# Heads' projections: Strassen over 16 K tiles in place of 14 for 27 pairs of column tiles

## Chip, core and metric

The kernel runs on one core of a Trainium2 chip. A core has a matrix engine (TensorE, PE on the profile's page; PEld is its loading of weights), three others that compute (VectorE or DVE, ScalarE or ACT, GpSimd or POOL), and SyncE (SP), which here issues the transfers of weights. Each engine runs its own list of instructions strictly in order and waits on semaphores for the others. TensorE writes its products into PSUM, a small memory of eight banks; everything else lies in SBUF, and the weights come from HBM by DMA. The metric is the time of one execution in device microseconds (us); lower is better.

## The reference

Two layers of a decoder with D = 2048, for 512 prompt tokens and 8 sample tokens, all in fp32. The part that matters here:

```python
h = rmsnorm(x, norm_g)
z = h @ w_in                          # 2048 x 8192
b_c, c_c, x_c, g_c, q, k, v, g_r = split_projection(z)
conv_y, new_buf = short_conv(c_c * x_c, conv_buf, conv_w)
y_conv = b_c * conv_y * silu(g_c)
q, k = rope(q), rope(k)               # 4 heads of 256
o, new_S = retention(q, k, v, ret_S, log_gamma)
y_ret = groupnorm(o) * gn_g * silu(g_r)
x = x + concat([y_conv, y_ret]) @ w_out
x = x + sigmoid(x @ w_pg) * (p_i @ w_ple)
```

After the two layers comes a final rmsnorm.

## The kernel before

**Tiling.** Activations lie transposed, as 16 K tiles of 128 partitions (features) by 520 columns (512 prompt tokens and 8 samples). The columns are used in two halves of 260, LEFT and RIGHT. A product with a weight matrix is made for two column tiles of the weights (256 output features) at a time; this is a *pair* (`pair`), and a layer has 32 pairs of `w_in` (16 for the heads: q, k, v and gate of four heads, then 16 for the convolution), 8 of `w_out` and 8 of `w_pg`.

**Three matmuls for one.** fp32 accuracy comes from splitting every operand into a high part, rounded to the engine's fast format, and the rest. `split_w` does it for weights: ScalarE writes the high part (L229) and VectorE the difference (L230). `mm3` then makes three matmuls (L247 to L249), each 128x128 weights by 260 columns.

**Strassen.** A pair has 2 x 16 weight tiles and 16 x 2 activation tiles (K tiles by halves). `plain` multiplies them directly: 16 x 2 x 2 x 3 = 192 matmuls. `strassen(x, src0, src1, s)` takes the first `s` K tiles as a 2 x 2 block problem (even and odd K tiles, two halves, two weight tiles), in Winograd's form with seven products of q = s / 2 tiles each in place of eight. The sums of activations, t1 to t4, are made once and kept (`operand_sums`, L413 to L416, then split in `split_sums`); the sums of weights are made for each pair on VectorE (`add`, L319: four sums of q tiles). The K tiles from `s` to 16, if any, are multiplied directly at the end of the pair: `parts` loads them (L222) and four `product` calls use them. In all a pair costs 7 x q x 3 + (16 - s) x 4 x 3 matmuls: 171 with s = 14, 168 with s = 16.

Banks of PSUM for pairs are five. A pair holds three (a, b, d) and, only when s < 16, a fourth, c, into which ScalarE copies b (`copy(... c, b)`, L307), so that the last K tiles can add to it. With s = 16 that copy goes to SBUF, and two of the later copies become sums on VectorE with one operand in PSUM.

**Weights on their way.** Raw weights land in a ring of 32 tiles of 128 columns (`raw_ring`), taken in steps of 8 tiles (steps of 4 for pieces of up to 4 tiles). A block of q tiles is loaded, summed and split in chunks of at most four tiles: with q = 7 as 3 + 4 (instructions of 384 and 512 columns), with q = 8 as 4 + 4. The last two K tiles of s = 14 come as two more loads of 256 columns. Split weights go into a second ring of 60 tiles (`split_ring`), which is how far ScalarE and VectorE can run ahead of TensorE.

**What sets the order.** The tables `HEADS` and `CONVS` give s for each pair of `w_in`, in the order in which the pairs run; `OUT_ROWS` and `GATES` do so for the rest. The host packs the weights by the same tables. A scheduler at build time orders the instructions of each engine, by priorities and its own estimate of times. Between a pair's products stand other steps: `rope` (L753 to L758), `silu`, the sample states (`sample_step`, L777 to L785) and, in pieces taken from the list `later`, retention itself (`steps`, L870 to L1001). `Operands.need` sees to it that a pair finds the sums of all its K tiles: `need(n)` builds until s / 2 sums are there. `fill` builds more of them when slots of SBUF are free.

Of the kernel before, what the change touches and what calls it, by code (L numbers as in the profile page):

```python
# [49 lines left out]
EARLY = 6  # L50


HEADS = [[0, 0, 0, 8] + [14] * 12, [0] + [14] * 15]
CONVS = [[14] * 2 + [16] * 13 + [14]] * 2
OUT_ROWS = [[0, 8, 16, 16, 16, 16, 16, 0]] * 2

# [135 lines left out]
def trunk_kernel(  # L192
# [370 lines left out]
    def norm_g(l, k):  # L563
        return vec[:, 16 * l + k : 16 * l + k + 1]
# [97 lines left out]
    def from_dram(src):  # L662
        def load(k):
            t = get()
            SIDE.dma_start(t, src[k])
            return t

        return load

    xs = []  # L670
    X = Operands(HEADS[0][2:] + CONVS[0], from_dram(xT), gain=lambda k: norm_g(0, k))
    X.todo = [t for t in ((i, False, True) for i in range(max(X.rows) // 2))]
# [43 lines left out]
    for l in range(DEPTH):  # L716
# [456 lines left out]
        if not tail:  # L1173
            X = Operands(HEADS[l + 1] + CONVS[l + 1], next_in, RESERVE_NEXT, gain=lambda k, l=l: norm_g(l + 1, k))
        for m in range(0, KT - tail, 2):
# [303 lines left out]
```

## Time and profile before

| | |
|---|---|
| runs | 2172.50, 2166.74, 2170.08 us; median 2170.08 |
| the profiled execution | 2172.46 us, its span 2170.4 us |
| granted TensorE clock over the span | 0.998 |
| ACT busy over the span | 1266.2 us (58%) |
| POOL busy over the span | 430.5 us (20%) |
| DMA over the span | 387.31 MB, mean 178 GB/s |

The profile is of one execution, and the 2.1 us between its time and its span lie before its first and after its last instruction. In the span the first layer's heads run until about 380 us and its convolution until about 700 us; the output and gate projections follow until about 1118 us, where the second layer's heads take up, until about 1466 us; its convolution ends at about 1780 us. A row of a group of instructions ends with their busy time, the mean of one in ns, and then the engine's idle time before them with what ended it. A row of the windows gives busy us of each engine in a stretch, with the number of instructions in brackets.

### The profile page before, as it was taken

To read this page: it belongs to the slowest core of one execution; us is meant where nothing else is said; L and a number is where in the kernel's file an instruction comes from. 1 tells how busy PE (TensorE), PEld (TensorE's weight loads), DVE (VectorE), ACT (ScalarE), POOL (GpSimd) and SP (SyncE) were. 2 spreads that over 40 slices of the span, in tenths; PEclk is the share of its full clock that TensorE was granted. 3 is DMA by queue.
4 is the path that set the end of the run, shared out by engine and by line. 5 is a ranking of instruction groups with operands and counts; after the bars stand their busy time and mean duration, and the time that the engine had idled before them with its cause. 6 is when DMAs were issued, how large, how long until landed. Compare 5 with 4: busy or idle time off the path is not lost. (4 is left out here: it accounts for less than half of the span.)

```text
span 2170.4 us, 48198 instructions
## 1 busy us (share of the span) xinstructions
PE 2148.5 (99%) x17861; PEld 2142.9 (99%) x17861; DVE 1895.7 (87%) x3849; ACT 1266.2 (58%) x2661; POOL 430.5 (20%) x746
## 2 busy tenths in 40 slices
PE   9999999999999999999999999999999999999998
PEld 9999999999999999999999999999999999999998
DVE  8889989898999987987897988989999998878884
ACT  8656556655555555655765655565655555456565
POOL 2313222211001211210212222231111022121011
PEclk9999999999999999999999999999999999999999
DMA  8556675545543645645645566665464455566455
GB/s 288 176 169 196 185 215 183 186 152 172 156 134 120 228 156 186 217 153 161 214 144 174 172 210 193 190 195 183 147 182 145 127 155 199 181 212 195 127 169 192
DMA packets 182861, 387.31 MB, mean 178 GB/s; under 512 B 25888, under 2 KB 56352, under 8 KB 182624
## 3 DMA queue, kind: packets, MB, share of 16 engines
q1 hardware_dynamic: 129136, 213.77, 31.8%
q0 software_dynamic: 53056, 169.84, 23.8%
q8 instruction: 140, 2.29, 0.4%
q14 instruction: 97, 0.79, 0.1%
q10 hardware_dynamic: 432, 0.61, 0.1%
HBM read 318.96 MB, written 65.15 MB: 177 GB/s over the span
## 5 line engine op out<-in xcount | busy, mean ns | idle before, releaser
L247 PE MATMUL ps_g<-slot,split 128*128 128x260 f32 x5465 | 1532.3, 284 | 9.7 <-ACT slot L307 3.4
L248 PE MATMUL ps_g<-slot,split 128*128 128x260 f32 x5465 | 1535.1, 283 | 0.3 <-DVE slot L555 0.3
L249 PE MATMUL ps_g<-slot,split 128*128 128x260 f32 x5461 | 1520.5, 283 | 0.5 <-DVE split L230 0.5
L229 ACT ACTIVATE split<-raw 128x512 fp32r<-128x512 f32 (+2 forms) x1347 | 778.2, 596 | 587.6 <-DVE raw L319 205.6
L247 PEld LDWEIGHTS ps_g<-slot,split 128*128 128x128 f32 x5465 | 1024.5, 188 | 12.9 <-ACT slot L307 4.2
L248 PEld LDWEIGHTS ps_g<-slot,split 128*128 128x128 f32 x5465 | 1029.3, 188 | 0.5 <-DVE slot L555 0.5
L249 PEld LDWEIGHTS ps_g<-slot,split 128*128 128x128 f32 x5461 | 1020.3, 188 | 0.8 <-DVE split L230 0.7
L230 DVE TENSOR_TENSOR split<-raw,split 128x512 fp32r<-128x512 f32 (+2 forms) x1346 | 844.1, 647 | 176.5 <-PE ps_g L248 85.4
L319 DVE TENSOR_TENSOR raw<-raw 128x512 f32<-128x512 f32 (+1 forms) x660 | 426.2, 656 | 28.1 <-DMA raw<-wi 18.4
L307 ACT ACTIVATE slot<-ps_g 128x260 f32<-128x260 f32 x336 | 127.2, 381 | 142.5 <-PE ps_g L249 127.2
L551 ACT ACTIVATE slot<-slot 128x520 fp32r<-128x520 f32 (+1 forms) x212 | 109.1, 562 | 41.8 <-DVE slot L414 10.2
L552 DVE TENSOR_TENSOR slot<-slot,slot 128x520 fp32r<-128x520 f32 (+1 forms) x212 | 122.9, 609 | 4.3 <-ACT slot L551 4.2
L782 POOL DMA_DIRECT2D o_rets<-slot x64 | 35.3, 552 | 350.6 <-DVE slot L781 131.8
L307 DVE TENSOR_TENSOR slot<-ps_g,slot 128x260 f32<-128x260 f32 x168 | 70.5, 421 | 7.3 <-PE ps_g L249 4.9
L870 POOL DMA_DIRECT2D slot<-hs x64 | 46.1, 723 | 126.5 <-DVE split L230 35.5
L815 POOL DMA_DIRECT2D hs<-slot x64 | 35.6, 556 | 137.9 <-DVE slot L756 59.6
L747 DVE TENSOR_TENSOR slot<-slot,slot 128x520 f32<-128x520 f32 x80 | 55.4, 692 | 4.6 <-DMA o_rets<-slot 3.7
L1059 POOL DMA_DIRECT2D slot<-x1s x76 | 40.8, 538 | 88.0 <-PE ps_g L249 28.3
L781 DVE SCALAR_TENSOR_TENSOR slot<-slot,vs,slot 128x256 f32<-128x256 f32 x128 | 55.9, 477 | 2.6 <-ACT slot L777 2.3
L1209 POOL DMA_DIRECT2D x2s<-slot x30 | 16.3, 545 | 203.4 <-DVE slot L1204 202.5
L771 POOL DMA_DIRECT2D slot<-sret x64 | 35.5, 555 | 106.4 <-ACT split L229 43.4
L772 POOL DMA_DIRECT2D slot<-kq x64 | 34.9, 547 | 109.2 <-DVE slot L877 20.5
(217 smaller groups left out, 1727.0 us busy)
## 6 DMA issues: line engine op xcount, KB each, us to landing
raw<-wi SPq DMA_DIRECT2D x377, 256.0 KB, 3.9
raw<-wo SPq DMA_DIRECT2D x128, 256.0 KB, 5.6
raw<-wg SPq DMA_DIRECT2D x122, 256.0 KB, 4.2
raw<-wi SPq DMA_DIRECT2D x136, 192.0 KB, 4.0
slot<-x1s POOLq DMA_DIRECT2D x76, 260.0 KB, 5.0
slot<-sret POOLq DMA_DIRECT2D x64, 256.0 KB, 4.0
hs<-slot POOLq DMA_DIRECT2D x64, 256.0 KB, 3.9
slot<-hs POOLq DMA_DIRECT2D x64, 256.0 KB, 5.1
```

The costliest lines, as they stand in the source:

```text
L229: S.activation(hi, raw, AF.Copy)
L230: V.tensor_tensor(lo, raw, F(hi), SUB)
L247: PE.matmul(out, wh, xh, start=start, stop=False, skip_group_check=more)
L248: PE.matmul(out, wh, xl, start=False, stop=False, skip_group_check=more)
L249: PE.matmul(out, wl, xh, start=False, stop=stop, skip_group_check=more)
L307: fn(*args)
L319: V.tensor_tensor(out[:, n], x[:, n], y[:, n], op)
L551: keep(S.activation(hi, src[:, n], AF.Copy))
L552: V.tensor_tensor(lo, src[:, n], F(hi), SUB)
L747: V.tensor_tensor(out[:, n], v, table[:, n], MUL)
L781: keep(V.scalar_tensor_tensor(st[:, c], k, vs[:, h, e, b : b + 1], st[:, c], MUL, ADD))
L870: SIDE.dma_start(t[:, :512].rearrange("p (m n) -> p m n", m=2), src)
```

## The change

One table is changed. In layer 0 the pairs 4 to 15 of the heads, in layer 1 the pairs 1 to 15, are computed with s = 16; 12 + 15 = 27 pairs.

```diff
-HEADS = [[0, 0, 0, 8] + [14] * 12, [0] + [14] * 15]
+HEADS = [[0, 0, 0, 8] + [16] * 12, [0] + [16] * 15]
 CONVS = [[14] * 2 + [16] * 13 + [14]] * 2
 OUT_ROWS = [[0, 8, 16, 16, 16, 16, 16, 0]] * 2
```

In the built program TensorE has 81 matmuls fewer (17746 for 17827), VectorE 54 instructions fewer (3797 for 3851), ScalarE 81 fewer (2585 for 2666), SyncE 54 loads fewer with the same bytes. Among the forms: the splits (L229, L230) of 256 columns go from 66 to 12 and those of 384 from 249 to 60 on each of the two engines, and those of 512 go up by 189; the sums of weights (L319) of 384 columns go from 140 to 32, those of 512 from 520 to 628; copies from PSUM to PSUM (L307) go from 121 to 94. The order of the convolutions, the output and the gate projections stays as it was but for a few rows at the seams.

On SyncE, where the first layer's heads begin (`raw<-wi` is a load of `w_in` into the ring), the rows of the difference are:

```order
 L222 DMA raw<-wi 128x512 x4
+L312 DMA raw<-wi 128x512 x96
+L312 DMA raw<-wi 128x384
+L312 DMA raw<-wi 128x512
 L312 DMA raw<-wi 128x384 x2
 L312 DMA raw<-wi 128x512 x2
 L312 DMA raw<-wi 128x384
-L312 DMA raw<-wi 128x512
-L312 DMA raw<-wi 128x384
-L312 DMA raw<-wi 128x512
-L222 DMA raw<-wi 128x256 x2
```

The mixed loads, with two of 256 columns at each pair's end (L222), have become 96 loads of 512 columns in a row, eight for each of the twelve pairs; the first two pairs of the convolution, which keep s = 14, follow with the old sizes.

On ScalarE, in the first layer beside retention's first state (`ps_st`, `decay`), where one pair ends and the next begins, before:

```order
L307 ACTIVATE ps_g<-ps_g 128x260
L954 ACTIVATE slot_178_2016<-ps_st,decay 128x512
L229 ACTIVATE split<-raw 128x512
L229 ACTIVATE split<-raw 128x384
L307 ACTIVATE ps_g<-ps_g 128x260
L229 ACTIVATE split<-raw 128x512
L989 ACTIVATE slot_179_2041<-ps_o,shift,rstp 128x256 x2
L777 ACTIVATE slot_174_1911<-slot_174_1911,vec 128x512
L229 ACTIVATE split<-raw 128x256 x2
L229 ACTIVATE split<-raw 128x384
L307 ACTIVATE slot_187_2082<-ps_g 128x260 x2
```

and of the change at the same place:

```order
L307 ACTIVATE ps_g<-ps_g 128x260
L229 ACTIVATE split<-raw 128x512 x2
L954 ACTIVATE slot_178_1994<-ps_st,decay 128x512
L229 ACTIVATE split<-raw 128x512 x2
L989 ACTIVATE slot_179_2019<-ps_o,shift,rstp 128x256 x2
L777 ACTIVATE slot_174_1915<-slot_174_1915,vec 128x512
L229 ACTIVATE split<-raw 128x512 x3
L307 ACTIVATE slot_187_2059<-ps_g 128x260 x2
L229 ACTIVATE split<-raw 128x512 x2
L307 ACTIVATE slot_188_2060<-ps_g 128x260
```

The second copy from bank to bank (b into c) and the two splits of 256 columns are gone from the pair's end; the copies of results into slots stand in the same order, among splits that are all of 512 columns.

On VectorE, before the first of the changed pairs, the eighth sum of activations moves. Before, it stands among the rotations of the first q and k (`slot_150` and `slot_151` are its two halves):

```order
L230 TENSOR_TENSOR split<-raw,split 128x512
L755 TENSOR_TENSOR slot_65_721<-slot_66_724,slot_70_734 128x520
L413 TENSOR_TENSOR slot_150_1583<-slot_148_1577 128x260
L415 TENSOR_TENSOR slot_151_1584<-slot_149_1579,slot_148_1577 128x260
L755 TENSOR_TENSOR slot_67_727<-slot_68_730,slot_70_734 128x520
```

and with the change it stands some thirty rows later, behind the transpose for the samples (L842), where the pair ahead of the first changed pair adds up its result (L307, out of bank c; `slot_141` and `slot_142` are the sum's halves):

```order
L413 TENSOR_TENSOR slot_141_1402<-slot_139_1396 128x260
L307 TENSOR_TENSOR slot_112_1109<-ps_g,slot_112_1109 128x260
L319 TENSOR_TENSOR raw<-raw 128x512
L230 TENSOR_TENSOR split<-raw,split 128x512
L414 TENSOR_TENSOR slot_141_1402<-slot_140_1398,slot_141_1402 128x260
L415 TENSOR_TENSOR slot_142_1403<-slot_140_1398,slot_139_1396 128x260
```

In the second layer the eighth sum keeps its place, before the rotation's tables are scaled (L729).

## Prediction

> **What bounds the kernel now.** I read the page's head first, then the chain of work that ended last.
>
> ```profile
> span 2170.4 us, 48198 instructions
> PE 2148.5 (99%) x17861; PEld 2142.9 (99%) x17861; DVE 1895.7 (87%) x3849; ACT 1266.2 (58%) x2661; POOL 430.5 (20%) x746
> PE 43%; DMA 2%; issue 2%; DVE 1%; ACT 1%; POOL 0%; DVEq 0%; POOLq 0%; ACTq 0%
> ```
>
> TensorE is busy for 99% of the span, and it is the largest share of the chain. A busy PE need not be a PE at its pace, so the second thing to read is how far apart its matmuls start: the timeline of TensorE in an undisturbed stretch.
>
> ```profile
> 299.83 0.28 PE L247 MATMUL ps_g<-slot,split 128*128 128x260 f32 x1
> 300.79 0.28 PE L249 MATMUL ps_g<-slot,split 128*128 128x260 f32 x1
> ```
>
> Eight matmuls start between these two: 0.96 / 8 = 0.120 us each, with no gap. That is the price of a matmul here, not the 0.28 us that one lasts, since they overlap. VectorE, at 87%, is the only other engine near its limit. Whether it or TensorE sets the pace is a question for each stage, so the third view is the busy time in windows (columns: PE, PEld, DVE, ACT, POOL, clock, DMA).
>
> ```profile
> 100.00:380.00 280.00, 280.00 (x2344) 280.00 (x2343) 252.74 (x565) 168.00 (x368) 76.47 (x133) 1.00 0.60 190
> 380.00:700.00 320.00, 319.26 (x2667) 319.09 (x2666) 290.95 (x586) 177.22 (x362) 46.23 (x70) 1.00 0.49 153
> 700.00:740.00 40.00, 36.03 (x284) 35.42 (x283) 38.16 (x82) 27.63 (x80) 13.20 (x25) 0.96 0.76 250
> 1118.00:1466.00 348.00, 346.00 (x2887) 345.00 (x2886) 306.58 (x673) 201.98 (x450) 90.33 (x155) 1.00 0.60 187
> 1466.00:1780.00 314.00, 313.56 (x2619) 313.02 (x2619) 289.75 (x581) 176.56 (x364) 45.80 (x70) 1.00 0.49 153
> ...
> 1700.00:1780.00 80.00, 80.00 (x672) 80.00 (x671) 75.49 (x155) 45.63 (x95) 10.73 (x10) 1.00 0.41 124
> ```
>
> The first and fourth rows are the heads of the two layers, where the changed pairs stand; the second and fifth are mostly convolution, which already runs 13 of its 16 pairs with s = 16. TensorE is full in all four. VectorE has 252.74 / 280 = 90.3% in the first heads and 306.58 / 348 = 88.1% in the second. **TensorE bounds the heads**, and VectorE has 27 and 41 us left there.
>
> **The change part by part.** *Matmuls.* A pair goes from 171 to 168, so 27 x 3 = 81 are removed, as the program's counts say. They stand at the pair's end in an unbroken row of matmuls: 81 x 0.120 = **-9.7 us**. [...] The measured spacing, 0.120 us, decides, and the sum goes by it.
>
> *VectorE and ScalarE.* The groups by form give the durations.
>
> ```profile
> L230 DVE TENSOR_TENSOR split<-raw,split 128x512 fp32r<-128x512 f32 x1031 | 690.9, 685 | 152.9 <-PE ps_g L248 81.9 <-ACT split L229 53.8 <-issue 7.2
> L230 DVE TENSOR_TENSOR split<-raw,split 128x384 fp32r<-128x384 f32 x249 | 136.1, 550 | 15.3 <-ACT split L229 8.0 <-PE ps_g L248 3.6 <-ACT slot L551 1.6
> L230 DVE TENSOR_TENSOR split<-raw,split 128x256 fp32r<-128x256 f32 x66 | 27.0, 417 | 8.3 <-ACT split L229 8.1
> L319 DVE TENSOR_TENSOR raw<-raw 128x512 f32<-128x512 f32 x520 | 351.9, 684 | 13.7 <-DMA raw<-wi 6.6 <-DMA raw<-wo 4.6
> L319 DVE TENSOR_TENSOR raw<-raw 128x384 f32<-128x384 f32 x140 | 76.9, 550 | 14.4 <-DMA raw<-wi 11.8 <-DMA raw<-wg 2.1
> ...
> L229 ACT ACTIVATE split<-raw 128x512 fp32r<-128x512 f32 x1032 | 632.8, 627 | 468.6 <-DVE raw L319 184.7 <-PE ps_g L249 181.2 <-PE ps_g L248 50.3
> L229 ACT ACTIVATE split<-raw 128x384 fp32r<-128x384 f32 x249 | 127.3, 518 | 77.7 <-PE ps_g L248 24.4 <-DVE raw L319 20.9 <-PE ps_g L249 17.9
> L229 ACT ACTIVATE split<-raw 128x256 fp32r<-128x256 f32 x66 | 27.3, 415 | 41.2 <-DMA raw<-wi 35.8 <-PE ps_g L248 3.0 <-PE ps_g L249 1.9
> L307 ACT ACTIVATE ps_g<-ps_g 128x260 f32<-128x260 f32 x121 | 45.1, 373 | 17.4 <-PE ps_g L249 16.9
> ```
>
> On each engine 189 splits of 384 columns become 512, and 54 of 256 go; on VectorE 108 sums of 384 also become 512. VectorE: 189 x (0.685 - 0.550) - 54 x 0.417 + 108 x (0.684 - 0.550) = 25.5 - 22.5 + 14.5 = **+17.5 us busy**, 0.65 a pair. ScalarE: 189 x 0.109 - 54 x 0.415 - 27 x 0.373 = 20.6 - 22.4 - 10.1 = -11.9 us; at 58% that is no bound. VectorE's instructions overlap a little when they follow each other:
>
> ```profile
> 1131.90 0.68 DVE L230 TENSOR_TENSOR split<-raw,split 128x512 fp32r<-128x512 f32 x1
> 1132.50 0.69 DVE L755 TENSOR_TENSOR slot<-slot,slot 128x520 f32<-128x520 f32 x1
> 1133.11 0.55 DVE L230 TENSOR_TENSOR split<-raw,split 128x384 fp32r<-128x384 f32 x1
> 1133.58 0.55 DVE L319 TENSOR_TENSOR raw<-raw 128x384 f32<-128x384 f32 x1
> ```
>
> From start to start it is 0.60 for 512 columns and 0.47 for 384, 0.08 less than the duration; a removed instruction then frees only 0.34. By these the work added is 297 x 0.13 - 54 x 0.34 = 20 us, so 17.5 is the lower end.
>
> Is there room? In the first heads VectorE goes to (252.74 + 12 x 0.65) / (280 - 12 x 0.36) = 260.5 / 275.7 = 94.5%, in the second to (306.58 + 15 x 0.65) / (348 - 15 x 0.36) = 316.3 / 342.6 = 92.3%. The nearest rows: at 92.3% the second convolution let TensorE wait 0.44 us in 314, and at 94.4% its last 80 us none. What hides the added work is VectorE's idle time, and the ring of 60 split tiles that smooths its bursts. Bounds for what TensorE pays: 0 by those rows, 17.5 if none of the idle can be used. I take **+1.0 us**, near the rows of the convolution, and a little over them because the heads come in bursts (rotations, gates, sample states).
>
> *The pair's end.* With s = 16 the late loads of the last K tiles and the copy into bank c are gone. What they do shows at 1270 us, in the second heads:
>
> ```profile
> 1269.92 0.42 ACT L229 ACTIVATE split<-raw 128x256 fp32r<-128x256 f32 x1 [1.37 <-DMA raw<-wi]
> 1270.87 0.37 ACT L307 ACTIVATE ps_g<-ps_g 128x260 f32<-128x260 f32 x1
> 1271.29 0.39 PE L247 MATMUL ps_g<-slot,split 128*128 128x260 f32 x1 [0.90 <-ACT ps_g L307]
> ...
> PE ps_g L247 <- ACT ps_g L307: 2.9, 4, 1.1
> PE ps_g L247 <- ACT ps_g L307: 1.8, 3, 0.9
> ```
>
> ScalarE sits 1.37 us before a split of 256 columns whose load is late; behind it in its queue is a copy between banks, and TensorE waits 0.90 us for that. The last two rows are such waits of TensorE in the whole span and in the second heads: 2.9 and 1.8 us. Of these only what hangs on the removed loads and the 27 copies goes: 0 to 1.8 us, and a loss is excluded by no row but would be a wait of the kind counted above. I take **-1.0 us**, half, since the copy from a into d stays.
>
> *Banks.* Two of five stay free with s = 16 instead of one, so the next pair starts its second product without waiting for a bank. The row of the second convolution (0.44 us lost) already contains that; nothing more is booked.
>
> *The eighth sum* of activations is now needed by the first changed pair. Its price is known:
>
> ```profile
> L413 DVE TENSOR_TENSOR slot<-slot 128x260 f32<-128x260 f32 x48 | 20.2, 422 | 7.5 <-DMA slot<-x1s 6.2 <-ACT slot L465 0.8 <-PE ps_g L249 0.3
> L552 DVE TENSOR_TENSOR slot<-slot,slot 128x520 fp32r<-128x520 f32 x148 | 99.0, 691 | 3.6 <-ACT slot L551 3.6
> ```
>
> Four steps of 0.42 and two splits of 0.69 are 3.1 us, paid before as well. In the first layer it stands behind the closing sum of the pair ahead. From there the order has ten VectorE rows to its first split, some 5 us at 0.34 to 0.60 each, while TensorE still has three products of that pair's last tiles, the first product of the new pair and seven tiles of its second: 36 + 24 + 21 = 81 matmuls, 9.7 us. So it is covered by 4.7 us; uncovered it would cost up to 3.1. In the second layer its place is unchanged. I book 0.
>
> Weights: the same bytes in 54 fewer loads; 0.
>
> Sum: -9.7 + 1.0 - 1.0 = **-9.7 us**. Against the profiled execution, 2172.46, that is 2162.8; it lies 2.4 above the median of the runs, 2170.08, from which the same sum gives 2160.4. A new median should lie near the latter; I say **2161.0**, leaning a little to the former.
>
> **The rivals.** *The gain is given back in waits.* VectorE's bursts make TensorE wait, in the first heads above all (94.5%). One wait of the size seen at 1271 us, 0.9 us, in each of the 12 pairs there: +10.8, so 2170.1 - 9.7 + 10.8 = 2171.2. For it: the row 700 to 740, where VectorE has 95.4% and TensorE lost 4 of 40 us. Against it: that row is a seam, with chains that the heads lack, and the 94.4% row lost nothing. Waits can cost more than themselves:
>
> ```profile
> 720.00:740.00 20.00, 17.11 (x128) 16.70 (x127) 18.16 (x39) 12.09 (x39) 5.59 (x11) 0.91 0.76 265
> 740.00:760.00 20.00, 20.00 (x169) 19.98 (x168) 16.18 (x33) 9.79 (x21) 3.94 (x8) 1.00 0.55 175
> PE ps_g L247 <- ACT split L229: 1.9, 1, 1.9
> ```
>
> Here 41 matmuls, 4.9 us, are missing against the next row, with 2.9 us of waits (20.00 - 17.11) and a granted clock of 0.91. [...] Chance 0.25.
>
> *VectorE becomes the bound: slower.* If its idle time in the heads cannot be used, because each idle stretch waits for something that TensorE needs too, its added work lengthens the stage: +17.5 us, with no gain from TensorE: 2187.6. It decides from the point where VectorE's 27 and 41 us of idle in the two stages stay what they are. Against it: in all stages with s = 16 VectorE works at 91 to 94% under a full TensorE, and the first row of its splits waits 81.9 us for TensorE, which is work done too early. Chance 0.06.
>
> *More than the sum.* All 2.0 us that TensorE lost in the second heads go and nothing is added: 2158.4. For it: VectorE's and ScalarE's waits for late loads (35.8 us before the 256 splits) go. Chance 0.12.
>
> *The change does nothing*, 2170: excluded by the counts of matmuls but for chance; 0.01. That leaves 0.56 for the forecast, 2157 to 2166.
>
> **How the numbers follow.** A measurement of this kernel tells about 0.3% from no change: 6.5 us, so faster is below 2163.6 and slower above 2176.6. Faster: nine tenths of the forecast and the better case, 0.50 + 0.12 = 0.62. Slower: the VectorE rival and a tenth of the waits, 0.06 + 0.02 = 0.08. The rest, 0.30, is the same. The range goes from the better case less the 3.3 us by which the lowest run lay under the median, 2155, rounded down to 2154, to the waits case plus half the runs' spread (2.9), 2174; it leaves out the slower rival.
>
> **What would show it.** Right: 81 matmuls fewer, 100 to 376 us and the second heads still with TensorE at 99% or more, VectorE at about 94 and 92% there, no splits of 256 columns in the heads and no wait of TensorE on a copy between banks behind one. Wrong: TensorE waiting on splits of VectorE in the heads, VectorE's idle there unchanged, a first changed pair that waits on the eighth sum, or new waits or a lower clock at the seams near 700 and 1780 us.

## The result and the profile after

The change is slower, by 0.8%. Its median is 2186.64 us (four runs, 2185.05 to 2187.76) against 2168.77 for the kernel before beside it (four runs, 2166.74 to 2172.5): a ratio of 1.008, 95% interval 1.0062 to 1.0097. The forecast was 2161.0 with a range of 2154 to 2174; one of the rivals, VectorE as the bound, had been worked out at 2187.6. The experiments below ask whether it came out right for its own reason.

The head of the page and the engines' shares of the chain that ended last, after:

```profile
span 2184.6 us, 47639 instructions
PE 2147.4 (98%) x17780; PEld 2137.7 (98%) x17780; DVE 1915.4 (88%) x3795; ACT 1257.1 (58%) x2580; POOL 431.9 (20%) x746
PE 74%; DMA 4%; DVE 3%; ACT 2%; issue 2%; POOL 0%; DVEq 0%; POOLq 0%; SPq 0%; ACTq 0%
```

The span grew by 14.2 us although 81 matmuls are gone (17861 to 17780). VectorE's busy time rose by 19.7. The page's 98% of TensorE hides the loss; the windows show it (columns: PE, PEld, DVE, ACT, POOL, clock, DMA share, GB/s):

```profile
100.00:380.00 280.00, 272.14 (x2249) 270.56 (x2248) 253.00 (x523) 158.70 (x325) 76.45 (x130) 0.99 0.58 187
380.00:700.00 320.00, 318.76 (x2660) 318.35 (x2659) 294.52 (x597) 179.71 (x368) 48.98 (x74) 1.00 0.50 154
700.00:740.00 40.00, 38.95 (x320) 38.32 (x319) 39.03 (x83) 29.25 (x83) 10.66 (x20) 1.00 0.72 249
1118.00:1466.00 348.00, 336.85 (x2765) 333.69 (x2764) 309.73 (x626) 190.72 (x390) 85.99 (x147) 0.99 0.57 180
1466.00:1780.00 314.00, 313.64 (x2622) 313.22 (x2621) 289.12 (x581) 175.58 (x363) 46.65 (x71) 1.00 0.49 155
```

TensorE now waits 7.9 us in the first heads (280.00 - 272.14; before 0) and 11.2 in the second (before 2.0); the convolutions wait 0.4 us more in all, and the seam at 700 us 2.9 less. The counts of matmuls show the whole loss: 95 and 122 fewer start in the two stages than before (2344 - 2249, 2887 - 2765), which at 0.120 us is 11.4 and 14.6 us. So 17.0 of these 26.0 us are new waits (7.9 and 9.1), and the rest are matmuls that start further apart; the granted clock is 0.99 in both stages, where it was 1.00. VectorE did not rise to the 94.5% and 92.3% of the forecast: it stands at 253.00 / 280 = 90.4% and 309.73 / 348 = 89.0%. Its idle time there is 27.0 and 38.3 us, where it was 27.3 and 41.4. **The added work did not go into VectorE's idle time. The stages became longer instead.**

What TensorE waits for, whole span (total, times, longest), after:

```profile
PE ps_g L247 <- ACT split L229: 10.2, 6, 3.4
PE ps_g L249 <- DVE split L230: 5.9, 7, 1.7
PE ps_g L247 <- ACT slot L307: 4.4, 6, 1.5
PE ps_g L247 <- ACT ps_g L307: 3.1, 2, 1.5
```

Waits on splits, 1.9 and 0.5 us before, are now 16.1. Most of them (10.2 us) name ScalarE, not VectorE. One place from the timeline shows why that doesn't acquit VectorE:

```profile
257.14 0.63 ACT L229 ACTIVATE split<-raw 128x512 fp32r<-128x512 f32 x1 [2.10 <-DMA raw<-wi]
257.80 0.69 DVE L230 TENSOR_TENSOR split<-raw,split 128x512 fp32r<-128x512 f32 x1 [0.95 <-ACT split L229]
...
257.82 0.39 PE L247 MATMUL ps_g<-slot,split 128*128 128x260 f32 x1 [3.44 <-ACT split L229]
```

TensorE waits for ScalarE, ScalarE for a load, and VectorE for ScalarE; the load itself was issued late, because its block is free only when a VectorE sum (L319) has read it: such a sum ended at 251.93 us, and SyncE issued a load at 251.96. It is a ring of engines, and the name at its end is that of the last link. The waits of ScalarE in the first heads (100 to 380 us) say the same:

```profile
ACT split L229 <- PE ps_g L249: 43.3, 38, 6.0
ACT split L229 <- DVE raw L319: 20.6, 17, 3.0
ACT split L229 <- DMA raw<-wi: 13.4, 7, 4.1
...
ACT slot L307 <- DMA hs<-slot: 4.5, 1, 4.5
```

Before, the lines of the splits were:

```profile
ACT split L229 <- PE ps_g L249: 19.1, 33, 1.8
ACT split L229 <- PE ps_g L248: 18.3, 28, 2.2
ACT split L229 <- DVE raw L319: 13.6, 16, 1.6
ACT split L229 <- DMA raw<-wi: 8.9, 6, 3.4
```

A split that waits for TensorE waits for a place in the split ring, which the matmuls of L248 or L249 read last. Together these two lines were 37.4 us, and they are 43.9 now (L248 stands at 0.6). The waits for VectorE's sums and for loads grew by half.

### The profile page after: what moved, and what is told of

Same layout as the page of the kernel before. It is cut to its first block, busy times and chain, and to the rows that moved or that the text cites. A ratio compares the mean times of both kernels' runs of the same rounds, so it can differ in the third digit from the quotient of the medians.

```text
span 2184.6 us, 47639 instructions
## 1 busy us (share of the span) xinstructions
PE 2147.4 (98%) x17780; PEld 2137.7 (98%) x17780; DVE 1915.4 (88%) x3795; ACT 1257.1 (58%) x2580; POOL 431.9 (20%) x746
## 4 chain that ended last, share of the span: by engine, by line
PE 74%; DMA 4%; DVE 3%; ACT 2%; issue 2%; POOL 0%; DVEq 0%; POOLq 0%; SPq 0%; ACTq 0%
PE ps_g L247 23%; PE ps_g L249 23%; PE ps_g L248 23%; DMA raw<-wi 2%; DVE split L230 1%; ACT split L229 1%; DMA o_rets<-slot 1%; DMA hs<-slot 1%; ACT slot L551 1%; DVE slot L552 0%; PE ps_p L247 0%; PE ps_p L249 0%; PE ps_p L248 0%; DVE raw L319 0%; DMA x2s<-slot 0%
## 5 line engine op out<-in xcount | busy, mean ns | idle before, releaser
L247 PE MATMUL ps_g<-slot,split 128*128 128x260 f32 x5434 | 1525.2, 284 | 20.7 <-ACT split L229 10.2
L248 PE MATMUL ps_g<-slot,split 128*128 128x260 f32 x5434 | 1528.1, 283 | 0.3 <-DVE slot L555 0.3
L249 PE MATMUL ps_g<-slot,split 128*128 128x260 f32 x5434 | 1515.8, 283 | 6.1 <-DVE split L230 5.9
L229 ACT ACTIVATE split<-raw 128x512 fp32r<-128x512 f32 (+1 forms) x1292 | 778.2, 620 | 608.4 <-PE ps_g L249 245.1
L249 PEld LDWEIGHTS ps_g<-slot,split 128*128 128x128 f32 x5434 | 1017.2, 189 | 8.2 <-DVE split L230 8.2
L248 PEld LDWEIGHTS ps_g<-slot,split 128*128 128x128 f32 x5434 | 1024.1, 189 | 0.5 <-DVE slot L555 0.5
L230 DVE TENSOR_TENSOR split<-raw,split 128x512 fp32r<-128x512 f32 (+1 forms) x1292 | 849.4, 675 | 182.8 <-PE ps_g L248 87.3
L319 DVE TENSOR_TENSOR raw<-raw 128x512 f32<-128x512 f32 (+1 forms) x660 | 439.7, 677 | 26.0 <-DMA raw<-wi 21.6
L307 ACT ACTIVATE slot<-ps_g 128x260 f32<-128x260 f32 x336 | 126.9, 383 | 141.3 <-PE ps_g L249 119.9
L307 DVE TENSOR_TENSOR slot<-ps_g,slot 128x260 f32<-128x260 f32 x168 | 70.6, 420 | 5.4 <-PE ps_g L249 3.5
```

The source lines that it names most:

```text
L229: S.activation(hi, raw, AF.Copy)
L230: V.tensor_tensor(lo, raw, F(hi), SUB)
L247: PE.matmul(out, wh, xh, start=start, stop=False, skip_group_check=more)
L248: PE.matmul(out, wh, xl, start=False, stop=False, skip_group_check=more)
L249: PE.matmul(out, wl, xh, start=False, stop=stop, skip_group_check=more)
L307: fn(*args)
```

## The experiments

Eighteen kernels were run. Each is compared with some runs of the kernel before on the same chip; "against before" is the difference of the two medians. The change itself stands at +17.9 us.

### Is it the late load, or a ring that is too small?

The block of `w12` in the raw ring is given back later, together with that of `w11` and behind it, so that the next pair's first load goes where `w11` lay:

```diff
-        raw_ring.put(w12)
         step(4)
...
-        raw_ring.put(w11)
+        raw_ring.put(w11, w12)
```

> The changed kernel, with w12's block of the raw ring given back together with w11's and behind it, so that the next pair's first block goes where w11 lay and not where w12 lay. No work is added or left out. Theory late loads (the next pair's first load waits for the sum that reads w12 last, and lands 4 us too late): the waits of TensorE at 257 and 1333 us go, and the time falls by 5 us or more, to 2182 or less. Theory VectorE (its 17.5 us of added work set the pace): within 3 us of the 2186.6 of the change. Theory split ring (chunks are split too near to their use, because the places they go to are freed late): within 3 us of it too.

2184.97 us, +16.0, ratio 1.007 (1.0055 to 1.0086). TensorE's waits in this run:

```profile
PE ps_g L247 <- ACT slot L307: 7.2, 8, 2.9
PE ps_g L249 <- DVE split L230: 5.5, 6, 1.7
...
PE ps_g L247 <- ACT split L229: 2.8, 2, 2.5
```

The wait on ScalarE's splits fell from 10.2 to 2.8 us, as it should, yet the time fell by 1.9 only (17.9 - 16.0): other waits rose in its place, that on copies out of PSUM from 4.4 to 7.2. In the heads TensorE still waits 6.8 and 8.3 us (before this edit 7.9 and 11.2). By these figures late loads are not the main part of the loss.

The same line moved in the kernel before, as a control for what a mere reordering costs:

> Control: the kernel before with the same order of giving back w12 and w11. In the heads s = 14 puts the late pieces of the last K tiles into w12's place, so theory late loads expects within 6 us of the kernel before, either way; the other theories expect no change.

2176.76 us, +7.8, ratio 1.0034 (1.0022 to 1.0046). An edit that adds no work costs 8 us here, so differences of this size between orders prove little by themselves. It also leaves open how much late loads cost: if the edit by itself costs the change as much as its control, the gain is not 1.9 us but 9.7, of the 27.6 that are to be explained (17.9 and the 9.7 us that the matmuls should have saved).

Rings of other sizes, with s = 16 (`RAW` 32 to 40 and `SPLIT` 60 to 56; then `SPLIT` 60 to 64):

> The changed kernel with a raw ring of 40 tiles (five blocks for a pair that uses four) and a ring of split weights of 56 tiles for 60. Theory late loads: the first load of a pair can start a whole product earlier, 2165 to 2178. Theory VectorE: 2187, no change. Theory split ring: the smaller ring makes it worse, 2190 or more.

> The changed kernel with a ring of split weights of 64 tiles for 60 (an even eight chunks of four tiles, high and low). Theory split ring: the waits on splits near 161, 166, 1237 and 1243 us go, 2170 to 2182. Theory VectorE: 2183 to 2187. Theory late loads: 2184 to 2188.

2199.06 us, +30.1, ratio 1.0135 (1.0118 to 1.0152), and 2183.94, +15.0, ratio 1.0065 (1.0048 to 1.0082). Four places fewer in the split ring, with a deeper ring of raw weights, cost 12 us; four more bring 3. The first run changed two rings, so it does not show which of them cost the 12 us; a larger split ring does not mend the loss. With 64 places the waits moved again:

```profile
PE ps_g L247 <- ACT slot L307: 14.4, 12, 2.3
...
PE ps_g L249 <- DVE split L230: 3.0, 6, 0.8
```

### Is it VectorE's work? Adding it to the kernel before

One VectorE instruction of 128x512 on a tile that nothing else uses, written into the middle of each of the 27 pairs (18.5 us in all), and then two:

```diff
+        def more_work():
+            for _ in range(1):
+                V.tensor_tensor(extra, extra, extra, MUL)
...
+            if X.rows[m // 2 - skipped] > 8:
+                middle.append(more_work)
```

> The kernel before (s = 14) with one more VectorE instruction of 128x512 in the middle of each of the 27 pairs: 27 x 0.685 = 18.5 us of added VectorE work on a tile that nothing reads, as much as the change adds; loads, ScalarE, matmuls and banks as before. Theory VectorE (its idle time in the heads cannot be used): 2169 + 18 = 2187, at least 2178. Theory structure (what the s = 16 pair lacks or orders otherwise, not the amount of VectorE work): 2166 to 2173.

> The same with two such instructions in each pair, 37 us of added VectorE work. Theory VectorE: 2206. Theory structure: under 2180.

2179.73 us, +10.1, ratio 1.0044 (1.003 to 1.0059), and 2192.48, +22.9, ratio 1.01 (1.0082 to 1.0117). But the scheduler did not leave the instructions in the pairs. Nothing waits for them, and it moved them to the front. In the run with one:

```profile
L806 DVE TENSOR_TENSOR extra<-extra x27: 678/685/696, 1.4 to 81.8; 128x512 f32<-128x512 f32 x27
```

The last two times are the first and the last start: all 27 started before 82 us, and none in the stretch of the changed pairs, from 100 us on, or in the second layer. With two a pair, the 54 ran from 1.4 to 176.6 us. So neither run prices the work where the change puts it. What they show is read from the windows, first before:

```profile
0.00:100.00 100.00, 97.14 (x780) 95.53 (x781) 84.74 (x166) 71.66 (x150) 30.06 (x61) 1.00 0.71 236
```

and with one instruction a pair:

```profile
0.00:100.00 100.00, 96.81 (x773) 95.05 (x774) 92.60 (x176) 66.87 (x139) 23.95 (x50) 1.00 0.66 215
100.00:380.00 280.00, 273.55 (x2274) 272.15 (x2273) 249.68 (x559) 164.50 (x365) 81.14 (x141) 1.00 0.61 193
1118.00:1466.00 348.00, 345.75 (x2878) 344.09 (x2877) 305.95 (x667) 199.36 (x447) 88.33 (x151) 1.00 0.59 184
```

Up to 100 us VectorE is busy 7.9 us longer, for 18.5 us of added work; so some of its other work was pushed on into the first heads. There it had 27 us idle, and it did not use them to catch up: it is busy for 249.68 of 280 us, no more than the 252.74 of the kernel before, and TensorE waits 6.5 us where it waited for nothing. The second heads, to which nothing was added, wait 2.3 us (before 2.0). So a VectorE that enters the first heads late stays late, and part of the idle time there is not to be had. How much a pair's own added work costs, these runs don't show.

### Is it VectorE's work? Taking it away

These kernels no longer compute the reference's output; they only show what the work costs. First, the sample states' reductions, 63 us of VectorE's work by their durations, in both kernels. In the trace of the kernel before, 74 of the 128 reductions (L785) run in the two heads' windows and the rest in the convolutions; the page's busy time of VectorE falls by 34.0 us in the change and 30.4 in the control, not by 63:

```diff
+    G.memset(osum, 1.0)
...
-            for e in range(2):
-                c = slice(256 * e, 256 * e + 256)
-                V.tensor_tensor_reduce(k, st[:, c], kb[:, :256], 1.0, 0.0, MUL, ADD, osum[:, e, h, b : b + 1])
```

> The changed kernel without the sample states' reductions over the key axis (the sample part of the output is left out): 128 instructions of 0.415 us and as many short reads of 0.08 us, about 63 us of VectorE work less, some 1.2 us for each pair of the heads, twice what the change adds there. Theory VectorE: the waits of TensorE in the heads go, 2160 to 2166. Theory structure: 2178 or more.

> Control: the kernel before without the same reductions. It waits only 2 us in the second heads and 2 more elsewhere in projections: 2163 to 2168 under both theories; what s16_less_vector lies under or over it is the change without VectorE's load: 9.7 us under by theory VectorE, over it by theory structure.

2166.06 us, -3.6, ratio 0.9981 (0.9969 to 0.9994), and for the control 2165.3, -4.3, ratio 0.9979 (0.997 to 0.9989). The change is no longer slower than its control: 0.8 us above it instead of 17.9. But it should now be 9.7 below. In the first heads of the change:

```profile
100.00:380.00 280.00, 278.06 (x2324) 277.64 (x2323) 252.91 (x475) 166.88 (x339) 79.06 (x134) 1.00 0.59 193
```

VectorE is as busy as ever, 252.91 us: what was taken away is filled at once with more of the pairs' work. TensorE still lacks 1.9 us here, and 5.0 in the second heads (343.00 of 348).

Then the work in the pair itself: one of the weights' sums, or two, left out of the heads' pairs.

```diff
...
-        add(w21, w12, w21, SUB)
+        if not cut:
+            add(w21, w12, w21, SUB)
...
```

> The change, with the weights' sum for the sixth product left out of every Strassen pair of the heads (two instructions of 128x512; the sixth product takes what stands in that block, so q, k, v and the gates are not the reference's). VectorE has 37 us less to do, 19 less than the kernel before has. Theory A, VectorE's load, which counts in the pair where the splits are due: no waits of TensorE in the heads, 2155 to 2160, 5 to 10 below its control. Theory C, a rest that does not hang on VectorE's load: 2162 to 2170, within 3 of its control.

> The control: the kernel before with the same sum left out of the same pairs (33 us less on VectorE). TensorE waits 2 us in its heads, so both theories give 2163 to 2168, near the 2165.3 of the control with less sample work.

> The change, with the sums for the sixth and the second product left out of the heads' pairs (73 us less on VectorE). Theory A: as fast as TensorE goes, 2153 to 2158, 8 to 11 below its control. Theory C: still within 3 of its control, 2162 to 2168.

> The control: the kernel before with the same two sums left out (67 us less on VectorE): 2162 to 2167, since TensorE has only some 2 us of waits in the heads to win back.

With one sum less: 2161.75 us, -8.1, ratio 0.9966 (0.9953 to 0.9979); control 2167.39, -2.4, ratio 0.999 (0.998 to 0.9999). With two less: 2161.92, -7.9, ratio 0.9964 (0.9952 to 0.9976); control 2165.48, -4.3, ratio 0.998 (0.9971 to 0.999). So one sum a pair, 36.7 us of VectorE's work by its durations, buys the change 26 us, and the control 2.4: the change goes from 17.9 slower than the kernel before to 8.1 faster, 5.6 below its control. The heads of the change without one sum:

```profile
100.00:380.00 280.00, 279.74 (x2338) 279.33 (x2337) 250.88 (x524) 166.32 (x339) 78.60 (x135) 1.00 0.60 194
1118.00:1466.00 348.00, 343.31 (x2864) 342.08 (x2863) 304.01 (x626) 198.51 (x410) 88.83 (x153) 1.00 0.57 186
```

In the first heads TensorE is full again; in the second it still waits 4.7 us. Theory A, VectorE's load, met its number of 5 to 10 below the control with one sum, though not its time of 2155 to 2160; with two the medians differ by 3.6 and not by 8 to 11. What TensorE itself does then agrees better, by the heads of those two pages (change, then control):

```profile
PE 2138.0 (99%) x17780; PEld 2131.8 (99%) x17780; DVE 1857.0 (86%) x3685; ACT 1260.6 (58%) x2580; POOL 431.3 (20%) x746
```

```profile
PE 2145.5 (99%) x17861; PEld 2140.9 (99%) x17861; DVE 1848.7 (85%) x3739; ACT 1275.1 (59%) x2661; POOL 430.1 (20%) x746
```

TensorE is busy 7.5 us less for 81 matmuls less. The gain on TensorE is there, and it comes out when VectorE has less to do: against its control the change goes from 17.9 us slower to 0.8 slower, 5.6 faster and 3.6 faster. Leaving out a sum takes a link out of the chain to the splits as well as work; the reductions, which stand outside that chain, bring back 17.1 us all the same.

### Are the result slots needed too early?

With s = 14 the second product's result waits in bank c; with s = 16 it goes to a result slot at once. In the change one of ScalarE's copies waits 4.5 us for a slot that is still being written out to hs, once in each layer (the last row above of its waits). Two runs were to remove that wait: the second product's result in a free bank again, and one slot more (`NSLOT` 75 to 76).

```diff
-        c = banks.get() if s < KT else None
+        c = banks.get() if s < KT or bank else None
...
             copy(z1[:, LEFT], a)
+            if s == KT:
+                plus(z1[:, RIGHT], c, z1[:, LEFT])
+                copy(z0[:, LEFT], d)
+                banks.put(c)
+                c = None
```

> The change, but in the heads' pairs the second product's result waits in a free fourth bank, as it did with s = 14, and not in the pair's result slot; after the fifth product it is added to that one's copy. One copy of 128x260 on ScalarE more in a pair, the first use of the second result slot later by three products; VectorE's work is the same. Theory A, VectorE's load alone: within 4 us of the change, 2181 to 2190, and the wait of 4.5 us of ScalarE's copies on a slot that is still being written out to hs (once in each layer, at 306 and 1382 us) may go without effect. Theory B, result slots that are needed earlier: this wait of 4.5 us falls under 2 in both layers, and the time falls by 5 to 10 us, to 2175 to 2180.

> The change with 76 slots in place of 75, which is all that fits. Theory B, slots asked for before their transfer out is done: the waits of ScalarE on hs and o_rets (14.9 us in the second heads) fall by half or more, and the time by 3 to 10 us, to 2175 to 2182. Theory A, VectorE's load alone: no change, 2182 to 2190. The order shifts by itself, which the control with another release order priced at up to 8 us, so a fall of less than that speaks for B only together with the shorter waits.

2188.86 us, +19.8, ratio 1.0089 (1.0071 to 1.0106), and 2214.23, +45.2, ratio 1.0212 (1.019 to 1.0235). With the bank, the second heads have this left of the wait, and the first none:

```profile
ACT slot L307 <- DMA hs<-slot: 2.2, 1, 2.2
```

But the same copies now wait for slots on another way out, the sample states' (`o_rets`), in the first heads

```profile
ACT slot L307 <- DMA o_rets<-slot: 6.3, 3, 2.7
```

and 6.4 us in the second, where these lines were 0.4 and 3.7 in the change. The copies' waits on slots were moved and not removed, so this run does not decide on theory B. The run with one slot more does remove most of them: the waits of all of ScalarE's instructions on both ways out fall from 11.8 to 4.0 us in the first heads (78 to 380 us) and from 16.3 to 2.2 in the second. Yet it is 27 us slower than the change, and TensorE's waits on ScalarE's splits grew:

```profile
PE ps_g L247 <- ACT split L229: 17.4, 13, 3.3
```

Fewer waits on slots brought no time, which speaks against theory B, as far as one order can. Why one slot more costs 27 us is open: it shifts which slot every later tile gets, and so the order, but no run takes that apart.

### Can it be mended?

GpSimd is busy for 20% of the span. It was given the sum for the sixth product, in both kernels:

```diff
...
-        add(w21, w12, w21, SUB)
+        add(w21, w12, w21, SUB, G if side else V)
...
```

> The change, but in the 27 changed pairs the sum for the sixth product (w12 - w21, two instructions of 128x512 a pair) runs on GpSimd: 54 x 0.68 = 36.7 us less on VectorE, in the pair itself and not in the steps between pairs. Theory A, VectorE's load: 2184 less 20 to 27, so 2157 to 2166, below the kernel before; VectorE at 90% of 100 to 380 us or less, TensorE at 279 of 280. Theory C, that a rest of some 10 us does not come from VectorE's load: no lower than 2166. Rival: GpSimd takes over 4 us for one such sum (no row shows one; its queue issues transfers as well), the sum comes late for the sixth product, and the time goes above 2186.

> The control: the kernel before with the same sum of its changed pairs on GpSimd (54 instructions, one of 512 and one of 384 columns less on VectorE in a pair, 33 us). TensorE has no waits in the heads to win back, so 2165 to 2170, and 0 to 5 below the kernel before. Theory A: the change with its sum on GpSimd lies 5 to 10 below this one; theory C: within 3 us of it. Rival: the sum comes late on GpSimd, both are slower by the same amount.

2210.9 us, +41.9, ratio 1.0206 (1.0169 to 1.0243); control 2200.39, +31.4, ratio 1.0141 (1.012 to 1.0162). The groups by form, in the run with s = 16:

```profile
L230 DVE TENSOR_TENSOR split<-raw,split 128x512 fp32r<-128x512 f32 x1220 | 842.3, 708 | 160.0 <-PE ps_g L248 86.8 <-ACT split L229 55.9 <-issue 7.2
...
L319 POOL TENSOR_TENSOR raw<-raw 128x512 f32<-128x512 f32 x55 | 93.1, 1695 | 95.8 <-DVE split L230 86.6 <-DVE shift L985 4.8 <-DVE mv L982 2.2
```

The rival held in another way than expected. One of a sum's two instructions takes 1.70 us on GpSimd in the mean, so the sum takes 3.4 and not over 4; ScalarE's splits wait 19.8 us for these sums. And VectorE's own splits rose from 684 to 708 ns, and its busy time from 1915.4 to 1935.0 us although 55 instructions had left it. The 75 splits of 512 columns that ran at the same time as one of GpSimd's sums took 1.05 us in the mean and up to 2.6, and of the others none took more than 0.70. Why they take longer there, the trace does not show.

Last, longer instructions: each weights' sum in one of 1024 columns instead of two of 512 (`CHA` 4 to 8). This changes every Strassen pair of the kernel, not the heads' alone.

> The change, with each weights' sum of a Strassen product in one VectorE instruction of 128x1024 instead of two of 128x512. By the starts in the trace of before, 0.60 us for 512 columns and 0.47 for 384, a fixed 0.08 us goes with each instruction: 108 fewer in the heads, 8.6 us less of VectorE's time there. At the 24.5 us that 36.7 us less bought, this is worth 5 to 6 us: 2179 to 2182. Rival: the first split of a product now waits for a sum of 1.1 us instead of 0.6, and the weights' second half must have landed: no gain or slower, 2186 to 2195.

> The control: the kernel before with the same long sums (896 columns in place of 512 and 384). TensorE has nearly no waits to win back in its heads: 2166 to 2170 if the longer sums come in time, above 2172 if the rival holds. A version that beats the kernel before would have to show under 2162.

2205.62 us, +35.0, ratio 1.0163 (1.0146 to 1.018); control 2192.28, +21.6, ratio 1.0098 (1.0083 to 1.0113). The sums by form with s = 16:

```profile
L319 DVE TENSOR_TENSOR raw<-raw 128x1024 f32<-128x1024 f32 x296 | 361.1, 1220 | 11.0 <-DMA raw<-wi 7.0 <-issue 1.2
```

One of 1.22 us stands for two of 0.68, and VectorE is busy for 1901.5 us in that run, 13.9 less than in the change. It is slower all the same, by 17 us with s = 16 (35.0 - 17.9) and by 22 with s = 14. The rival's account fits this, that the first split of a product has to wait for the whole sum; it was not tried by itself. No version that computes the reference beat the kernel before.

## Why the prediction was wrong, step by step

**The matmuls** were right in kind: 81 went. With VectorE relieved by two sums, TensorE was busy 7.5 us less than its control; the medians showed 3.6 to 5.6 us of the 9.7. The rest of the 9.7 was never seen in a time.

**VectorE's added work** was right as an amount: 17.5 us busy or 20 by the starts, measured 19.7 for the whole page. The two groups show its parts, 189 splits and 108 sums of 512 columns more than before:

```profile
L230 DVE TENSOR_TENSOR split<-raw,split 128x512 fp32r<-128x512 f32 x1220 | 813.8, 684 | 172.6 <-PE ps_g L248 86.3 <-ACT split L229 63.7 <-issue 6.2
L319 DVE TENSOR_TENSOR raw<-raw 128x512 f32<-128x512 f32 x628 | 422.9, 683 | 23.1 <-DMA raw<-wi 18.8 <-DMA raw<-wo 1.4
```

**What it costs is the step that failed**: "What hides the added work is VectorE's idle time, and the ring of 60 split tiles that smooths its bursts", booked at +1.0 us. The room was read off the convolution, where TensorE waited 0.44 us in 314 beside a VectorE at 92.3% and not at all in 80 beside one at 94.4%; the heads did not offer it. In the first heads VectorE was between 246 and 255 of 280 us busy in every run that made TensorE wait more than 1 us there, those with GpSimd and with long sums included, and the kernel before was at 252.74 already. The upper bound for this term, 17.5, was too low as well: against a time with 81 matmuls less, the change paid 27.6 us (17.9 + 9.7). The counts of matmuls place 26.0 of them in the two heads. That this loss hangs on VectorE's work is shown by taking work away: three ways of it bring back 17.1, 23.5 and 21.5 us against their controls. An edit that adds no work moved a time by 8 us, and one slot more by 27, so each of these alone would prove less than the three together.

**The rival "VectorE becomes the bound"** got the time (2187.6, measured 2186.64) and its condition: VectorE's idle in the two stages stayed what it was. It had been given 6 in 100. That its price is right to 1 us is partly luck. It counts one us of time for one of work and no gain from TensorE; the runs show a loss of 27.6 us for 17.5 to 20 us of work, less the 9.7 of the matmuls. At the opening, ahead of the pairs, the extra instructions cost 0.55 us for one us of work (10.1 / 18.5), and the second lot 0.69 (12.8 / 18.5). Why the change's work costs more than its own length is open. Part of it is that 9.0 of the 26.0 us in the two stages are no waits but matmuls that start further apart, at a granted clock of 0.99 where it was 1.00. Further, this work sits in the chain from sum to split to split to matmul; and with s = 16 the row of matmuls at a pair's end, which asks little of VectorE, is gone. The long sums speak for the chain, since they lower VectorE's work and still lose; the reductions, which are outside it, speak for the load. No run tells these apart.

**The pair's end**, -1.0 us: not seen. The waits on copies between banks were 2.9 us before and are 3.1, with other copies. The splits of 256 columns are gone from the heads' pairs, and with them the wait of 0.90 us at 1271 us; in the second heads another copy makes TensorE wait 1.5 us, where these waits were 1.8.

**Banks, weights and the eighth sum**, 0: no run speaks against it. From 78 us to 160, around the first changed pair, TensorE has one wait, of 1.5 us, on a copy between banks and not on an operand.

**The waits rival** (2171.2) named the right sign, "TensorE waiting on splits", and a size of 0.9 us a pair in the first heads alone; the waits there are 7.9 us, but in the second heads 11.2, which it did not count.

## What to carry to other kernels

Idle time of an engine is room only if the same stage has been seen to use it: a busier stage of another kind proves nothing. Taking work away, in the change and in a control, tells more than adding it: padding that nothing waits for goes where the scheduler likes, so look in the trace for where it ran before its price is read. The same holds for a wait that an edit is to remove: look whether another of its kind has taken its place. If taking one wait away makes another engine's wait grow by nearly as much, as with the release order, the rings and the slots here, the named waits are symptoms, and a busy time that stays the same from run to run can point to the engine behind them. Where several engines feed each other, how long one link takes can matter more than its sum of work: fewer, longer sums took 13.9 us of busy time from VectorE here, and the time rose by 17.

## What the runs showed of the hardware

After a wait of 2.74 us TensorE's matmuls started further apart for some 3.5 us. In the second heads of the change (windows of 20 us):

```profile
1320.00:1340.00 20.00, 17.20 (x130) 16.79 (x129) 17.23 (x38) 9.48 (x21) 7.28 (x12) 0.91 0.63 201
1340.00:1360.00 20.00, 20.00 (x170) 20.00 (x170) 16.82 (x36) 12.30 (x25) 3.65 (x7) 1.00 0.51 176
```

The wait of 2.74 us, the longest in the first row, ends at 1333.87. From 1334.81 to 1337.63 the matmuls start 0.22 us apart, and from 1337.78 on 0.12, as before the wait. In all, 40 matmuls are missing against the next row, 4.8 us at 0.120, for 2.8 us without work. So about 2 us were lost on top of the wait, and the granted clock was 0.91 in that row and 0.57 from 1333.80 to 1337.00. From 720 to 740 us in the kernel before it was 0.91 too, beside a longest wait of 1.95 us.

With sums of weights on GpSimd, a VectorE split of 512 columns that ran beside one took 1.05 us in the mean, and one that did not 0.69.

An edit of the order that adds no work cost 8 us on this kernel, and one slot more in the pool 27. The order is found by a scheduler from such numbers, and a single comparison of two orders does not price what was meant to differ.
